# Address distance between TensorE's two operands in a decoder trunk: 64 bytes against 256 and 128, and the heads' outputs in the weights' class

## The chip, the cores and the metric

The kernel runs on one core of a Trainium2 chip. The time is that of one execution on the device, in microseconds; the median of three executions is given. One further execution was profiled, and all rows below come from it.

## The reference

Two post-norm layers on 512 tokens of width 1024, all in float32. Each layer is a half-step SwiGLU feed-forward network (FFN, hidden width 2816), a token mixer, a cross attention into 256 memory tokens, and a second FFN. Each of the four parts ends with a layer norm of `alpha * x + part`. The mixer of layer 0 is differential attention, that of layer 1 a causal pooling.

```python
for i in range(DEPTH):                                     # DEPTH = 2
    x = layer_norm(a * x + 0.5 * swiglu_ffn(x, ...), ...)
    h = diff_attention(x, ...) if i == 0 else pool_mixer(x, ...)
    x = layer_norm(a * x + h, ...)
    x = layer_norm(a * x + memory_cross_attention(x, mem, ...), ...)
    x = layer_norm(a * x + 0.5 * swiglu_ffn(x, ...), ...)
```

Differential attention has 8 heads with two 64-wide halves of queries and keys each, a rotary embedding, and for each head `softmax(first) - lambda * softmax(second)` times the values, normed per head, then a projection by `w_o`. The pooling mixer subtracts x from means over 2, 4, 8 or 16 past tokens and multiplies each group of 256 columns by its own 256x256 matrix. Cross attention has 4 heads of width 256 and a projection by `wo`.

## The kernel before

**One product is three passes.** TensorE works on float32r operands. Every float32 operand is split into a high part and a low part (`split`: ScalarE copies, VectorE subtracts), and a product is three matmul instructions: high by high, high by low, low by high. `mm3` issues them, its lines 220, 221 and 222. A matmul has a stationary operand, 128 by 128, that is loaded first, and a moving one of 128, 256 or 512 columns that streams through. In `mm3(out, w, x)` the stationary one is `w` and the moving one `x`. The profile names a matmul by output, moving tile, stationary tile: `q<-xh,wh` moves xh over stationary wh.

**Which operand is which.** In projections of x to transposed outputs (q, k of attention, xq of cross attention, the FFN's first products) the split weights wh and wl are stationary and the transposed activations xh and xl move. In products that give tokens as rows (v, pv, the pooling's products, the output projections in `to_tokens`) the activations or the heads' outputs oT are stationary and the weights move. `to_tokens` makes eight outputs (two halves of the width, four blocks of 128 tokens) of eight k steps each; the first four k steps take weights in wh and wl, the last four, in the last round, in tiles of other names that have become free: qk, low and p in attention, q and kv in cross attention.

**Where tiles lie.** All memory is laid out by pools that are opened one behind another, so that an address is the sum of what lies ahead. `run` opens the constants, the tokens X0 to X3 and small tiles, pads to 480 modulo 512 (`LINE`), and then opens `xt` with xh and xl. Nearly every tile is a multiple of 512 bytes per partition, so what is opened next starts at the same remainder. A stage opens its weights' pools by `stage_pools`, and ahead of wh a pad of `APART` = 64 bytes (`to_w`): the weights' class. Then `phase_pool` opens the stage's own tiles in the order of its arguments; the mark `_x` among them is a pad of 512 - 64 bytes (`to_x`), behind which tiles are again in x's class. Ahead of `_x` lie, in attention, low, rt, a, p, o and qk; behind it v, oT and mask. In the cross attentions pT, p and kv lie ahead (p and kv of the second are pools of its stage, kv in the weights' class), and q, oT and gb behind. In the pooling p, pw and gb lie ahead, pooled and sq behind. The memory's transposed tiles lie in x's class in both layers. X0 to X3 start at 160 modulo 512.

**What sets the order.** The order of TensorE's instructions is written out: `weave` runs a main generator (projections) and lets a side generator (scores, softmax, values of earlier heads) in by an estimated clock, and the Tile scheduler keeps a program order on each engine and adds the waits. Attention: `da_main` makes v, q and k head by head, `da_side` the scores (`sc`), the mixed and turned probabilities (`pt`) and the values (`po`, lines 1210 and 1211). Cross attention: `xa_main` makes memory keys (`pk`), memory values (`pv`) and queries (`xq`), `xa_head` scores (`xs`) and outputs (`xo`). Pooling: `pp` and the group products, which like those of `to_tokens` are named `ps`. Transposes (line 506 and others) take their data as stationary operand and move the identity.

The layer norm of a token block (`ln_token`, lines 380 to 395) reads two rows of gains, loaded in tiles of the phase (`gain`): hr and sr in the FFN, v in attention, gb in the cross attentions.

Of the kernel before, what the change touches and what calls it, by code (L numbers as in the profile page):

```python
# [58 lines left out]
TURNS = ((1, 2), (0, 3))  # L59


APART, ROUND, LINE = 64, 512, 480


INV_FREQ_BITS = (
# [54 lines left out]
class Trunk:  # L120
    def __init__(self, tc, a, out, upto=8):
        self.tc, self.nc, self.a, self.out, self.upto = tc, tc.nc, a, out, upto
        self.side, self.late, self.gates = [], [], []
        self.ln_next_gb, self.kv_bufs = None, 8


    def warm(self, tile, bank, n):
# [32 lines left out]

    def to_x(self, ctx):

        self.pad(ctx, ROUND - APART)

    def to_w(self, ctx):

        self.pad(ctx, APART)

    @contextmanager
    def phase_pool(self, gain, spare, **bufs):  # L170
# [1425 lines left out]
            yield from self.xa_head(*self.heads[h][1])  # L1596

    def cross_attention(self, layer, ln):
        bufs = dict(q=8, oT=10, gb=2)
        if layer == 0:  # L1600
            self.kv, self.keys = [], []
            late, mem = self.side_pool("mem"), self.side_pool("mem")
            with self.other_pools():
                self.stage["mem"], self.stage["late"] = mem, late
                with self.phase_pool(("gb", "gb"), "p", pT=6, p=4, kv=8, _x=0, **bufs):
                    self.kvp = self.phase["kv"]
                    with self.tc.high_priority():
                        self.load_memory("p")
                    self.turn_banks = None
                    self.xa(layer, ln)  # L1610
            self.close_side()
            self.close_side()
        else:
            with self.later, self.phase_pool(("gb", "gb"), "p", pT=6, p=4, _x=0, **bufs):
                self.xa(layer, ln)

    def xa(self, layer, ln):
# [51 lines left out]
        self.side.pop().__exit__(None, None, None)  # L1669

    def ffn_pools(self):
        return self.stage_pools(4, dict(ra=4, rc=3), ("wh", "wl", "ra", "rc"))

    def other_pools(self, order=("wh", "wl", "raw")):
# [19 lines left out]
            self.ffn(layer, 1, ln)  # L1694

    def mixer(self, layer, ln):
        if layer == 0:
            bufs = dict(low=4, rt=2, a=4, p=8, o=2, qk=8, _x=0, v=4, oT=11, mask=1)
            with self.other_pools(), self.phase_pool(("v", "v"), "rt", **bufs):
                self.diff_attention(layer, ln)  # L1700
            self.close_side()
        else:
            self.later = ExitStack()
            self.later.enter_context(self.stage_pools(4, dict(raw=2), ("wh", "wl", "mem", "p", "raw")))
            self.to_w(self.later)
            self.kvp = self.later.enter_context(self.pool("kv"))
            bufs = dict(p=4, pw=1, gb=2, _x=0, pooled=16, sq=1)
            with self.phase_pool(("gb", "gb"), "sq", **bufs):
                side = self.pool_mixer(layer, ln)
                with self.tc.high_priority():  # L1710
                    self.load_memory()
                w = self.a["xa_wkv"][layer]
                raws = [self.raw_cols(w, c) for c in (0, D)]
                self.pool_bias()
                next(side)
                self.kv, self.keys, self.kv_bufs = [], [], 10
                self.weave(self.early_kv(layer, ln, 2, raws), side, 850, 8500)
            self.close_side()
# [46 lines left out]
```

## Time and profile before

| | us |
|---|---|
| median of three executions | 1913.4 |
| lowest and highest | 1912.26 and 1915.36 |
| span of the profiled execution | 1913.0 |
| TensorE busy in it | 1894.9 |
| VectorE busy | 1550.6 |
| ScalarE busy | 1003.8 |
| attention, 339 to 580 us | 241 |
| first cross attention, 580 to 744 us | 164 |
| pooling and second cross attention, 1395 to 1582 us | 187 |

The four FFNs and the turns between stages fill the rest. In the rows of the profile, PE is TensorE's matmul, PEld its load of stationary operands, DVE VectorE, ACT ScalarE. A row that groups instructions gives line, engine, operation, output and inputs, shapes and count; behind the bar stand the busy time in us, the mean duration of one in ns, and the engine's idle time ahead of them. A row of the timeline starts with start and duration in us. The ends of matmuls are modelled, so that the step from one start to the next is what counts, not the share of busy time.

### The profile page before, as it was taken

Reading aid. Unit: us, or ns where it says so; the run is one execution under the profiler, and the core shown is the slowest. Engines: PE = TensorE matmul, PEld = TensorE weight load, DVE = VectorE, ACT = ScalarE, POOL = GpSimd, SP = SyncE. Lnnn points to the kernel's source line nnn. Section 1 sums busy time; section 2 is a strip of 40 time slices with the busy share of each in tenths; the row PEclk is TensorE's granted clock in tenths of the full one; section 3 lists DMA queues with packets and bytes.
Section 4 is the critical chain, followed back from the end, with each engine's and each line's share of the span. In section 5 each row is a group of like instructions: output and inputs, shape, how many; then the busy total and the mean of one; then the engine's idle time right before and its main releaser. Section 6 shows DMA issues by size and latency. Waiting matters only on the chain.

```text
span 1913.0 us, 32564 instructions
## 1 busy us (share of the span) xinstructions
PE 1894.9 (99%) x13136; PEld 1733.1 (91%) x13136; DVE 1550.6 (81%) x2250; ACT 1003.8 (52%) x1546; POOL 317.3 (17%) x274
## 2 busy tenths in 40 slices
PE   9999999999999999999999999999999999999998
PEld 8999998888878888999998999999899889999997
DVE  7888889888867558889888988898787568898886
ACT  6555554566645435645554655455455436555552
POOL 3112120111110001221220311212130012211210
PEclk9999999999999999999999999999999999999999
DMA  9978772323225327987785687878344438877861
GB/s 248 216 166 187 166 146 82 91 67 89 89 67 155 111 66 198 182 179 162 144 192 179 109 179 165 183 163 184 111 133 133 134 87 171 178 159 166 188 132 56
DMA packets 246743, 277.96 MB, mean 145 GB/s; under 512 B 8256, under 2 KB 212544, under 8 KB 246592
## 3 DMA queue, kind: packets, MB, share of 16 engines
q0 software_dynamic: 92928, 92.29, 31.5%
q1 hardware_dynamic: 153664, 183.59, 30.0%
q8 instruction: 103, 1.69, 0.4%
q14 instruction: 48, 0.39, 0.1%
HBM read 273.75 MB, written 2.10 MB: 144 GB/s over the span
## 4 chain that ended last, share of the span: by engine, by line
PE 85%; DVE 10%; ACT 2%; DMA 1%; issue 1%; POOL 1%; SPq 0%; DVEq 0%; ACTq 0%; POOLq 0%
PE x L221 7%; PE x L220 7%; PE x L222 7%; PE ps L220 4%; PE z L221 4%; PE z L220 4%; PE z L222 4%; PE ps L222 4%; PE ps L221 4%; PE px L222 2%; PE px L220 2%; PE px L221 2%; PE pt L506 2%; PE y L222 2%; PE x L757 2%; PE xq L222 2%
## 5 line engine op out<-in xcount | busy, mean ns | idle before, releaser
L725 POOL DMA_DIRECT2D ra<-in_ffn_w_in_dram x132 | 170.7, 1314 | 982.3 <-DVE wl L732 966.5
L730 ACT CAST wh<-ra 128x1024 fp32r<-128x1024 f32 x176 | 185.1, 1053 | 208.0 <-PE x L221 63.3
L732 DVE TENSOR_TENSOR wl<-ra,wh 128x1024 fp32r<-128x1024 f32 x176 | 214.4, 1223 | 66.5 <-ACT wh L730 66.1
L220 PE MATMUL x<-xe,wh 128*128 128x256 f32 x704 | 195.0, 277 | 0.0
L221 PE MATMUL x<-xe,wh 128*128 128x256 f32 x704 | 194.8, 277 | 0.0
L222 PE MATMUL x<-xe,wl 128*128 128x256 f32 x704 | 194.8, 277 | 0.0
L730 ACT CAST wh<-rc 128x1024 fp32r<-128x1024 f32 x132 | 139.0, 1053 | 102.4 <-PE x L221 41.6
L135 ACT CAST wh<-b 128x1024 fp32r<-128x1024 f32 x112 | 117.8, 1052 | 130.4 <-PE x L221 66.1
L732 DVE TENSOR_TENSOR wl<-rc,wh 128x1024 fp32r<-128x1024 f32 x132 | 160.3, 1222 | 25.5 <-ACT wh L730 25.5
L136 DVE TENSOR_TENSOR wl<-b,wh 128x1024 fp32r<-128x1024 f32 x112 | 136.9, 1222 | 41.0 <-ACT wh L135 41.0
L220 PE MATMUL x<-xh,wh 128*128 128x256 f32 x536 | 148.7, 277 | 0.0
L221 PE MATMUL x<-xl,wh 128*128 128x256 f32 x536 | 148.3, 277 | 0.0
L222 PE MATMUL x<-xh,wl 128*128 128x256 f32 x536 | 148.3, 277 | 0.0
L220 PEld LDWEIGHTS x<-xe,wh 128*128 128x128 f32 x704 | 132.4, 188 | 1.3
L221 PEld LDWEIGHTS x<-xe,wh 128*128 128x128 f32 x704 | 132.3, 188 | 1.3
L222 PEld LDWEIGHTS x<-xe,wl 128*128 128x128 f32 x704 | 132.2, 188 | 0.0
L136 DVE TENSOR_TENSOR wl<-raw,wh 128x1024 fp32r<-128x1024 f32 x64 | 82.4, 1296 | 41.1 <-ACT wh L135 40.5
L221 PEld LDWEIGHTS x<-xl,wh 128*128 128x128 f32 x536 | 100.8, 188 | 0.7
L220 PEld LDWEIGHTS x<-xh,wh 128*128 128x128 f32 x536 | 100.7, 188 | 0.7
L222 PEld LDWEIGHTS x<-xh,wl 128*128 128x128 f32 x536 | 100.6, 188 | 0.0
L135 ACT CAST wh<-raw 128x1024 fp32r<-128x1024 f32 x64 | 66.4, 1049 | 61.0 <-PE xq L221 19.1
L220 PE MATMUL z<-xe,wh 128*128 128x256 f32 x352 | 97.5, 277 | 0.0
(447 smaller groups left out, 6266.0 us busy)
## 6 DMA issues: line engine op xcount, KB each, us to landing
ra<-in_ffn_w_in_dram POOLq DMA_DIRECT2D x132, 512.0 KB, 7.0
rc<-in_ffn_w_in_dram SPq DMA_DIRECT2D x88, 512.0 KB, 5.8
b<-in_ffn_w_out_dram SPq DMA_DIRECT2D x76, 512.0 KB, 4.8
ra<-in_ffn_w_in_dram SPq DMA_DIRECT2D x44, 512.0 KB, 4.7
rc<-in_ffn_w_in_dram POOLq DMA_DIRECT2D x44, 512.0 KB, 7.8
raw<-in_xa_wkv_dram SPq DMA_DIRECT2D x16, 1024.0 KB, 5.4
raw<-in_da_w_qkv_dram SPq DMA_DIRECT2D x16, 512.0 KB, 5.2
raw<-in_xa_wq_dram SPq DMA_DIRECT2D x8, 1024.0 KB, 5.7
```

Source lines behind the costliest of these rows:

```text
L135: self.nc.scalar.copy(hi, src),
L136: self.nc.vector.tensor_sub(lo, src, hi.bitcast(F32)),
L220: self.first_mm = mm(out, w[0], x[0], start=start, stop=False, skip_group_check=again)
L221: mm(out, w[0], x[1], start=False, stop=False, skip_group_check=again)
L222: self.last_mm = mm(out, w[1], x[0], start=False, stop=stop, skip_group_check=again)
L506: self.turns = [self.nc.tensor.transpose(pt[:, j], b, self.ident) for j, b in enumerate(blocks)]
L725: nc.gpsimd.dma_start(t, source(*block), accum_op=ALU.add)
L730: hi = nc.scalar.copy(v[0], raw)
L732: lo = nc.vector.tensor_sub(v[1], raw, v[0].bitcast(F32))
L757: self.last_mm = nc.tensor.matmul(ps[:, j], v[i][:, k, j * P : (j + 1) * P], x[l][:, k], start=n == i == l == 0, stop=n == 7 and i == 1, s ...
```

## The change

The distance between the classes becomes a value of the stage: 64 bytes in the FFNs as before, 256 in attention and the first cross attention, 128 in the pooling and the second cross attention. The pad ahead of the weights has that size, and the pad back to x's class 512 bytes less it. Besides, oT is opened ahead of `_x` and not behind it, in attention and in both cross attentions, so that the heads' outputs lie in the weights' class; v (attention) and q (cross attentions) come to lie behind oT.

```diff
-APART, ROUND, LINE = 64, 512, 480
+APART, ROUND, LINE = dict(ffn=64, da=256, xa=(256, 128)), 512, 480
...
+        self.apart = APART["ffn"]
...
-        self.pad(ctx, ROUND - APART)
+        self.pad(ctx, ROUND - self.apart)
...
-        self.pad(ctx, APART)
+        self.pad(ctx, self.apart)
...
     def cross_attention(self, layer, ln):
-        bufs = dict(q=8, oT=10, gb=2)
+        bufs, self.apart = dict(_x=0, q=8, gb=2), APART["xa"][layer]
...
-                with self.phase_pool(("gb", "gb"), "p", pT=6, p=4, kv=8, _x=0, **bufs):
+                with self.phase_pool(("gb", "gb"), "p", pT=6, p=4, kv=8, oT=10, **bufs):
...
-            with self.later, self.phase_pool(("gb", "gb"), "p", pT=6, p=4, _x=0, **bufs):
+            with self.later, self.phase_pool(("gb", "gb"), "p", pT=6, p=4, oT=10, **bufs):
...
     def ffn_pools(self):
+        self.apart = APART["ffn"]
...
     def mixer(self, layer, ln):
+        self.apart = APART["xa"][1] if layer else APART["da"]
         if layer == 0:
-            bufs = dict(low=4, rt=2, a=4, p=8, o=2, qk=8, _x=0, v=4, oT=11, mask=1)
+            bufs = dict(low=4, rt=2, a=4, p=8, o=2, qk=8, oT=11, _x=0, v=4, mask=1)
```

No instruction is added or taken out, and none changes its shape.

## The prediction

> **What bounds the kernel now.** I read the page's head first, then the stages that the change touches (a table by windows), then single matmuls in order of time, then groups of matmuls by operands and shape.
>
> ```profile
> span 1913.0 us, 32564 instructions
> PE 1894.9 (99%) x13136; PEld 1733.1 (91%) x13136; DVE 1550.6 (81%) x2250; ACT 1003.8 (52%) x1546; POOL 317.3 (17%) x274
> PEclk9999999999999999999999999999999999999999
> PE 85%; DVE 10%; ACT 2%; DMA 1%; issue 1%; POOL 1%; SPq 0%; DVEq 0%; ACTq 0%; POOLq 0%
> ```
>
> TensorE is busy 99% of the span at its full granted clock, and 85% of the chain that ended last is its own. Time comes or goes only as its passes (one matmul instruction each) follow each other faster or slower. Attention runs from 339 to 580 us, the first cross attention to 744, pool and second cross attention from 1395 to 1582:
>
> ```profile
> 339.00:580.00 241.00, 236.44 (x1473) 200.76 (x1471) 190.90 (x470) 136.82 (x362) 40.69 (x54) 1.00 0.27 81
> 580.00:744.00 164.00, 163.38 (x977) 142.70 (x976) 98.40 (x156) 70.01 (x132) 7.25 (x6) 1.00 0.46 136
> 1395.00:1582.00 187.00, 186.06 (x1212) 167.60 (x1211) 131.21 (x204) 85.80 (x159) 21.62 (x15) 1.00 0.41 124
> ```
>
> Behind each window stand its length and TensorE's busy time: these 592 us are TensorE's too. The FFN stages keep their 64 bytes, so I cost them at nothing.
>
> The timeline shows what addresses can touch (start, duration, engine, line):
>
> ```profile
> 399.97 0.39 PE L220 MATMUL q<-xh,wh 128*128 128x512 f32 x1
> 399.97 0.19 PEld L221 LDWEIGHTS q<-xl,wh 128*128 128x128 f32 x1
> ...
> 419.75 0.39 PE L220 MATMUL k<-xh,wh 128*128 128x512 f32 x1
> ...
> 422.78 0.40 PE L221 MATMUL k<-xl,wh 128*128 128x512 f32 x1
> ```
>
> While a pass streams its moving operand (the first name behind the arrow), the load of the next pass's stationary operand (the second) begins: both read SBUF at once. What the change sets is their distance, the next stationary start less the present moving start, modulo 512. All slices of 128 columns are 512 bytes long, so it is one number for a pair of tiles. By the order and sizes of the pools, x's class starts at 480 modulo 512 and the weights' class 64 further on.
>
> The 13 steps from 419.75 to 422.78 take 233 ns each, at recorded durations that alternate between 0.39 and 0.40. A duration is the step plus some 163 ns, so differences of mean durations are differences of steps. The wide passes (512 columns), mean ns behind the bar; I take the second and third pass of each triple (L221, L222), since the first holds waits:
>
> ```profile
> L221 PE MATMUL q<-xl,wh 128*128 128x512 f32 x64 | 25.3, 396 | 0.0
> L222 PE MATMUL k<-xh,wl 128*128 128x512 f32 x64 | 25.3, 395 | 0.0
> L221 PE MATMUL xq<-xl,wh 128*128 128x512 f32 x112 | 44.2, 395 | 0.0
> L221 PE MATMUL ps<-wl,oT 128*128 128x512 f32 x96 | 37.7, 393 | 0.0
> L222 PE MATMUL ps<-wh,oT 128*128 128x512 f32 x96 | 37.7, 392 | 0.0
> L221 PE MATMUL ps<-q,oT 128*128 128x512 f32 x32 | 12.5, 390 | 0.0
> L222 PE MATMUL ps<-q,oT 128*128 128x512 f32 x32 | 12.4, 391 | 0.0
> L221 PE MATMUL ps<-ha,xe 128*128 128x512 f32 x30 | 11.7, 389 | 0.0
> L222 PE MATMUL ps<-ha,xe 128*128 128x512 f32 x1 | 0.4, 400 | 0.0
> L222 PE MATMUL ps<-kv,oT 128*128 128x512 f32 x1 | 0.4, 392 | 0.0
> ```
>
> Where x moves and weights are loaded (q, k, xq) the distance is +64: 395 to 396 ns. Where weights move and heads' outputs are loaded (wh or wl with oT) it is -64: 392 to 393. Where both lie in one class (q with oT, ha with xe) it is 0: 389 to 391. The last two rows are single passes followed by the load of a token tile X, which starts at 160: there the distance is +192 (ha with xe, 400) and +128 (kv with oT, 392). So distance costs up to 11 ns a pass. No pass of 512 or 256 columns with fp32 operands shows a distance of 256.
>
> The Trainium skill, page "TensorE: Matmul & The Clock Gate", section "Step-by-step: what each phase is for", says that TensorE reads moving and stationary operands through two independent ports, and that loading the next weights takes no read bandwidth from the running matmul. By it the sum below would be 0; the rows above speak against it.
>
> The narrow passes (256 columns):
>
> ```profile
> L221 PE MATMUL x<-xe,wh 128*128 128x256 f32 x704 | 194.8, 277 | 0.0
> L221 PE MATMUL v<-wl,xh 128*128 128x256 f32 x128 | 35.8, 280 | 0.0
> L221 PE MATMUL pv<-wl,mem2h 128*128 128x256 f32 x32 | 8.9, 278 | 0.0
> L221 PE MATMUL xs<-kv,q 128*128 128x256 f32 x64 | 17.8, 278 | 0.0
> L221 PE MATMUL ps<-wl,pooled 128*128 128x256 f32 x32 | 9.0, 282 | 0.0
> L221 PE MATMUL pk<-mem2l,wh 128*128 128x256 f32 x32 | 8.9, 278 | 0.0
> L221 PE MATMUL xq<-xl,wh 128*128 128x256 f32 x32 | 9.0, 282 | 0.0
> L222 PE MATMUL ps<-hb,xe 128*128 128x256 f32 x8 | 2.3, 284 | 0.0
> ```
>
> and two stretches of pk in the timeline:
>
> ```profile
> 605.84 0.28 PE L220 MATMUL pk<-mem4h,wh 128*128 128x256 f32 x1
> 606.90 0.28 PE L220 MATMUL pk<-mem6h,wh 128*128 128x256 f32 x1
> ...
> 635.84 0.28 PE L220 MATMUL pk<-mem6h,wh 128*128 128x256 f32 x1
> 636.97 0.28 PE L221 MATMUL pk<-mem2l,wh 128*128 128x256 f32 x1
> ```
>
> Among the groups the order is another one: +64 is best in the FFN (277), -64 gives 278 to 282, and 0, the best for wide passes, is worst (284). The timeline warns against a finer reading: the same operands at +64 run nine steps in 1.06 us (118 ns) at 606 us and ten in 1.13 (113 ns) at 636. A stretch of narrow passes falls into one of two paces and stays there.
>
> **The change part by part.** Durations are from the profiled execution, 1913.0 us, against the 1913.4 of the median; I subtract from the median.
>
> Heads' outputs into the weights' class. to_tokens makes 3 x 8 x 8 x 3 = 576 wide passes in the three stages. In 480 of them (all of attention's, and wh, wl and kv in both cross attentions) moving and stationary now share a class: from -64 to 0. From 392.5 to 390.3 is -2.2 ns, x 480 = -1.1 us; bounds 0 and -3.5 ns (to 389), 0 to -1.7 us.
>
> The other 96, those of the tiles q, go from 0 to +256 or +128. Between 389 and 400 I take 393.5, +3 ns, near the 392 row: +0.3 us (bounds -0.1 to +0.9).
>
> q, k and xq: 192 + 192 in attention and 192 in the first cross attention go from +64 to +256, 144 in the second to +128: 720 wide passes at 395.4. Bounds are the best and the worst row, 389 and 400: -4.6 us to +3.3 us. I take 391.5. For +128 that is the row of 392. For 256 nothing is measured; it is the furthest apart that two starts can be modulo 512, and three of the five measured distances lie at 389 to 393. -3.9 x 720 = -2.8 us.
>
> The narrow passes: 384 of v, 384 of pv, 192 of xs and 96 of pooled leave -64 for 256 or -128; 384 of pk and 96 of xq leave +64 for +256 or +128. 1536 passes at 279.3 in the mean of their rows, between 277 and 284: -3.5 us to +7.2 us. Since pace depends on how a stretch is entered, I take little, -0.5 ns, near the bulk of rows at 278 to 280: -0.8 us.
>
> ```profile
> L1210 PE MATMUL po<-v,a 128*128 128x256 f32 x80 | 20.0, 312 | 0.0
> L1211 PE MATMUL po<-v,a 128*128 128x128 f32 x80 | 17.8, 223 | 0.0
> ```
>
> ```profile
> 343.12 1.28 DVE L395 SCALAR_TENSOR_TENSOR X<-X,rstd,sr 128x1024 f32<-128x1024 f32 x1
> 345.42 0.59 ACT L135 CAST v<-v 128x512 fp32r<-128x512 f32 x1 [0.72 <-PE v L222]
> ```
>
> po goes from +64 to +256 in 160 passes, too few to matter: 0, at 5 ns either way 0.8 us. Scores (q and k in one class) and xo (pT and kv in one class) keep distance 0.
>
> Tiles also move. In attention oT now lies ahead of v, so v lands 22 KB higher, where the FFN kept its norm's gains (tiles sr and hr). The first write of v on ScalarE would wait for the last read of sr on VectorE; that read ends at 344.40 and the write starts at 345.42, so it costs nothing with 1.0 us to spare. Were that cover gone, ScalarE's split of the weights behind it would come late, and TensorE with it, by at most the norm's 1.28 us. In the cross attentions q and oT change places over tiles read for the last time some 10 us earlier or more. No instruction, DMA or wait is added.
>
> Sum: -1.1 + 0.3 - 2.8 - 0.8 = -4.4 us, 1909.0.
>
> **The rivals.** First, all passes reach the best rows: -1.7 - 0.1 - 4.6 - 3.5 = -9.9, 1903.5. For it: 277 and 389 exist under load. Against: no distance gives both.
>
> Second, no change. Either distances count modulo 256 only: then 256 acts as 0, 576 wide passes gain 5.1 ns (-2.9), 864 narrow ones (v, pk, pv and xs of the first two stages) go to 284, +5 ns (+4.3), and with -1.1 for the heads' outputs it is +0.3, 1913.7. Or address distance is not the cause of the steps, or the pads don't produce it: 1913.4. For the former: the narrow and wide orders oppose each other at 0. Against: +192 and -64 would be the same, and they show 400 and 392. Against the latter: the same moving tile, ha, takes 389 or 400. The latter is what the two-port rule of the Trainium skill, page "TensorE: Matmul & The Clock Gate", comes to; the trace does not agree, by these 11 ns.
>
> Third, slower: the weight load sets the pace of narrow passes. A recorded load (0.19 above) is longer than the step of 113 to 120, so a load that is held up delays the next pass at once, while a wide pass has twice the time to hide it. If both new distances hold it up as 0 does now, 1536 passes go to 284: +7.2, and with wide passes unimproved +7.2 - 1.1 + 0.3 = +6.4, 1919.8. It decides once narrow passes lose 0.5 ns in the mean without a gain in the wide ones, or 2.3 ns with it. For it: 284 at 0. Against: 113 ns steps occur at +64 whatever runs beside.
>
> **How the numbers follow.** Forecast 0.50, first rival 0.12, second 0.26 (0.06 of it for steps that addresses do not set), third 0.12. A change of 0.2%, 3.8 us, is about what can be told from none. The forecast's own range is -7 to -1.5 us, two thirds of it beyond 3.8: faster 0.33 + 0.12 = 0.45, same 0.17 + 0.26 = 0.43, slower 0.12. The range takes in the first rival, the second and the forecast and leaves out the third: 1903.5 to 1914.5; the forecast alone 1906.4 to 1911.9.
>
> **What would show it.** In the groups of the changed kernel: wh and wl with oT at 389 to 391; q, k, xq at 391 to 392, not 395; pk, pv, v, xs at 277 to 280. The three windows should be shorter by about 2.5 us (attention), 1 (first cross attention) and 1 (second). Narrow rows at 282 to 285 would mean the third rival; wide rows still at 395 the second. A gap ahead of the first v copy would mean the moved tiles cost.

## The result: 1923.6 us, slower by 0.6%

| | before | after |
|---|---|---|
| median, us | 1913.1 | 1923.57 |
| lowest and highest | 1910.59 and 1915.36 | 1922.39 and 1925.2 |
| ratio, 95% interval | | 1.0058 [1.0046, 1.0070] |
| span of the profiled execution | 1913.0 | 1923.4 |
| attention, first pass of v to first of pk | 241.0 | 247.9 |
| first cross attention, from there to the first FFN pass | 164.2 | 168.2 |
| the two FFNs between | 650.7 | 650.8 |
| pooling and second cross attention | 186.7 | 187.2 |

The forecast was 1909.0, with a range from 1903.5 to 1914.5. The change costs some 11 us, and nearly all of it lies in attention and the first cross attention. (The stages grow by 11.5 us and the span by 10.4, since the first FFN, in which nothing was changed, took 1.3 us less in this execution; over the runs below it took 336.5 to 340.7.) The head of the page after:

```profile
span 1923.4 us, 32565 instructions
PE 1897.3 (99%) x13136; PEld 1739.9 (90%) x13136; DVE 1551.1 (81%) x2250; ACT 1003.7 (52%) x1546; POOL 317.4 (17%) x274
PEclk9999999999998999999999999999999999999999
```

TensorE's busy time rose by 2.4 us only, while the span rose by 10.4: most of the loss is idle time. And one slice of the granted clock, the thirteenth (577 to 625 us), shows an 8 where before it showed 9. Both point to the turn between attention and cross attention. The stages by windows (length, TensorE's busy time, and so on to the clock, DMA's share and GB/s):

```profile
337.90:585.80 247.90, 235.62 (x1471) 201.33 (x1468) 197.31 (x477) 138.50 (x366) 41.85 (x55) 0.99 0.27 84
585.80:754.00 168.20, 166.54 (x977) 147.68 (x977) 92.78 (x148) 68.65 (x128) 6.56 (x6) 0.98 0.42 126
```

In attention 12.3 us are now without a pass, 4.6 before. The timeline of before and then of after at that turn:

```profile
579.53 0.60 PE L1452 MATMUL pt<-ident,p 128*128 128x128 f32 x4
579.57 0.59 ACT L135 CAST mem4h<-pt 128x512 fp32r<-128x512 f32 x1
...
580.21 0.38 PE L220 MATMUL pk<-mem4h,wh 128*128 128x256 f32 x1
```

```profile
578.12 0.60 PE L1453 MATMUL pt<-ident,p 128*128 128x128 f32 x4
...
582.48 1.28 DVE L394 SCALAR_TENSOR_TENSOR X<-X,mean,v 128x1024 f32<-128x1024 f32 x1
...
583.86 1.28 DVE L396 SCALAR_TENSOR_TENSOR X<-X,rstd,v 128x1024 f32<-128x1024 f32 x1
585.18 0.58 ACT L136 CAST mem4h<-pt 128x512 fp32r<-128x512 f32 x1 [3.38 <-DVE X L396]
...
585.82 0.58 PE L221 MATMUL pk<-mem4h,wh 128*128 128x256 f32 x1 [7.10 <-ACT mem4h L136]
...
591.20 0.41 PE L222 MATMUL pk<-mem2l,wh 128*128 128x256 f32 x1
591.41 0.41 PE L223 MATMUL pk<-mem2h,wl 128*128 128x256 f32 x1
591.62 0.37 PE L221 MATMUL pk<-mem4h,wh 128*128 128x256 f32 x1
591.83 0.28 PE L222 MATMUL pk<-mem4l,wh 128*128 128x256 f32 x1
591.95 0.29 PE L223 MATMUL pk<-mem4h,wl 128*128 128x256 f32 x1
```

The cross attention begins with the memory's transposed tiles: TensorE turns the memory (pt), ScalarE copies the high part (mem4h), and pk multiplies it. Before, the copy starts 0.04 us after the transposes do. After, it starts 7.06 us after them, and the row says what released it: VectorE's line 396, the end of the last token block's norm, which reads the gains in tiles named v. The addresses say why. The memory's tiles are laid from the far end of SBUF: mem0h from 212960, mem4h from 221152. Before, oT filled 199648 to 222176, and v, with the gains in it, ended at 199648. After, v lies behind oT: the gains g from 205792 and b from 218080 to 222176. So mem4h may not be written until b has been read for the last time. The scheduler moved the copies behind the whole norm of the last token block (before, the first step of that norm on ScalarE came 3.4 us after the first copy), and TensorE stood still for 7.10 us.

The second loss follows. The passes behind the gap start 0.21 us apart, and from 591.83 on 0.12: for nearly 6 us TensorE ran at half its pace, on 24 passes or so, 24 x 0.09 = 2.2 us. The granted clock (the third number from the end) shows it in this window:

```profile
581.60:591.80 10.20, 5.83 (x25) 5.54 (x26) 7.08 (x8) 3.35 (x7) 1.08 (x1) 0.50 0.89 305
```

The clock fell to half 2.9 us after the end of the last transpose and came back 10.2 us later; the 8 in its row is this. What else the cross attention lost of its 4.0 us is a wait of 1.5 us ahead of a pass of kv with oT, which is 0 to 0.6 us in the three other runs of this order (e2, e5, e6), and the passes' own steps, below. The Trainium skill, page "TensorE: Matmul & The Clock Gate", section "HAM oscillation — how this bites in real kernels", tells of TensorE falling to half rate after an idle gap of over some 3.4 us; the trace agrees as to the half rate, with a gap of 7.10 us and steps of 0.21 against 0.12, but here the clock fell before 3.4 us had passed, at 2.9.

What the change was about can be read from the groups of after, the second and third pass of a triple (now L222 and L223):

```profile
L222 PE MATMUL xq<-xl,wh 128*128 128x512 f32 x112 | 43.9, 392 | 0.0
...
L222 PE MATMUL ps<-wl,oT 128*128 128x512 f32 x96 | 37.6, 391 | 0.0
...
L222 PE MATMUL v<-wl,xh 128*128 128x256 f32 x128 | 36.2, 283 | 0.0
...
L223 PE MATMUL k<-xh,wl 128*128 128x512 f32 x64 | 25.2, 393 | 0.0
L222 PE MATMUL q<-xl,wh 128*128 128x512 f32 x64 | 25.1, 392 | 0.0
...
L222 PE MATMUL xs<-kv,q 128*128 128x256 f32 x64 | 18.1, 282 | 0.0
...
L223 PE MATMUL ps<-q,oT 128*128 128x512 f32 x32 | 12.6, 393 | 0.0
...
L222 PE MATMUL ps<-wl,pooled 128*128 128x256 f32 x32 | 9.1, 285 | 0.0
...
L222 PE MATMUL pv<-wl,mem2h 128*128 128x256 f32 x32 | 9.0, 282 | 0.0
```

The wide passes came near the forecast: q, k and xq at 391 to 393, not 395 to 396. The mean of xq hides two stages, though: by windows it went from 395 and 397 to 390 and 391 in the first cross attention (256 bytes), and only from 394 and 395 to 394 in the second (128 bytes). The narrow ones did not: v went from 280 to 283, xs and pv from 278 to 282, pooled from 282 to 285.

### The profile page after: what moved, and what is told of

It reads as the page before. It is cut to its first block, busy times and chain, and to the rows that moved or that the text cites. A ratio compares the mean times of both kernels' runs of the same rounds, so it can differ in the third digit from the quotient of the medians.

```text
span 1923.4 us, 32565 instructions
## 1 busy us (share of the span) xinstructions
PE 1897.3 (99%) x13136; PEld 1739.9 (90%) x13136; DVE 1551.1 (81%) x2250; ACT 1003.7 (52%) x1546; POOL 317.4 (17%) x274
## 4 chain that ended last, share of the span: by engine, by line
PE 85%; DVE 9%; ACT 2%; DMA 2%; issue 1%; POOL 1%; SPq 0%; DVEq 0%; ACTq 0%; POOLq 0%
PE x L222 7%; PE x L221 7%; PE x L223 7%; PE z L222 4%; PE z L221 4%; PE z L223 4%; PE ps L221 4%; PE ps L223 4%; PE ps L222 4%; PE px L221 2%; PE px L223 2%; PE px L222 2%; PE y L223 2%; PE pt L507 2%; PE xq L221 2%; PE xq L223 2%
## 5 line engine op out<-in xcount | busy, mean ns | idle before, releaser
L222 PE MATMUL x<-xe,wh 128*128 128x256 f32 x704 | 194.8, 277 | 0.0
L223 PE MATMUL x<-xe,wl 128*128 128x256 f32 x704 | 194.8, 277 | 0.0
L136 ACT CAST wh<-b 128x1024 fp32r<-128x1024 f32 x112 | 117.8, 1052 | 131.5 <-PE x L222 67.0
L222 PE MATMUL x<-xl,wh 128*128 128x256 f32 x536 | 148.4, 277 | 0.0
L223 PE MATMUL x<-xh,wl 128*128 128x256 f32 x536 | 148.4, 277 | 0.0
L222 PEld LDWEIGHTS x<-xe,wh 128*128 128x128 f32 x704 | 132.3, 188 | 1.4
L223 PEld LDWEIGHTS x<-xe,wl 128*128 128x128 f32 x704 | 132.2, 188 | 0.0
L222 PEld LDWEIGHTS x<-xl,wh 128*128 128x128 f32 x536 | 100.7, 188 | 0.7
L223 PEld LDWEIGHTS x<-xh,wl 128*128 128x128 f32 x536 | 100.6, 188 | 0.0
```

Source lines behind the costliest of these rows:

```text
L136: self.nc.scalar.copy(hi, src),
L222: mm(out, w[0], x[1], start=False, stop=False, skip_group_check=again)
L223: self.last_mm = mm(out, w[1], x[0], start=False, stop=stop, skip_group_check=again)
```

## The experiments

Two theories at the start. **Wait:** the tiles' new order costs the 7 us gap and the half pace behind it, and distances nearly cancel. **Distance:** the new distances themselves make passes slower, and the gap is only where it shows.

| run | what it is | ratio to before, 95% interval | attention | first cross attention |
|---|---|---|---|---|
| change | | 1.0058 [1.0046, 1.0070] | 247.9 | 168.2 |
| e1_v_low | change, v below oT | 1.0007 [0.9998, 1.0015] | 240.9 | 164.7 |
| e2_order_alone | change's order, 64 bytes | 1.0049 [1.0035, 1.0062] | 247.9 | 165.6 |
| e3_distance_alone | change's distances, old order | 1.0013 [1.0004, 1.0021] | 241.0 | 165.3 |
| e4_layer0_256 | e1, 64 bytes in layer 1 | 1.0005 [0.9997, 1.0014] | 240.9 | 166.5 |
| e5_gains_swapped | change, g and b changed over | 1.0045 [1.0032, 1.0059] | 246.5 | 166.8 |
| e6_warm_wait | change, TensorE busy in the gap | 1.0041 [1.0028, 1.0053] | 248.0 | 165.0 |
| e8_all64_v_low | e1 with 64 bytes | 1.0000 [0.9991, 1.0008] | 241.0 | 164.2 |
| e9_192 | e8 with 192 bytes | 1.0005 [0.9996, 1.0014] | 239.9 | 164.5 |
| e10_192_ffn | e9, FFN's ha and hb moved | 1.0090 [1.0076, 1.0104] | 240.2 | 163.8 |

**e1_v_low** keeps the new distances and oT in the weights' class, but lays v where nobody needs the room early; `_w` is a pad back to the weights' class.

```diff
-            bufs = dict(low=4, rt=2, a=4, p=8, o=2, qk=8, oT=11, _x=0, v=4, mask=1)
+            bufs = dict(low=4, rt=2, a=4, p=8, o=2, _x=0, v=4, _w=0, qk=8, oT=11, mask=1)
```

> The change with one more pad, so that v (which also holds the gains of attention's norm) lies below qk and oT and away from the memory's transposed tiles; classes and distances are those of the change in all stages. Wait theory (the 10 us are a wait of the memory's first transposed tile for the norm's last reading of the gains in v, 7 us, and passes at half clock behind it, 2 us): both go, 1914 us, and the first pk pass starts within 1.5 us of attention's last transposes. Distance theory (narrow passes at 256 and 128 cost the 10 us): 1922 to 1924, unchanged.

1914.06 us, ratio 1.0007 [0.9998, 1.0015]. The gap is gone; the turn in the timeline:

```profile
576.70 0.60 PE L1455 MATMUL pt<-ident,p 128*128 128x128 f32 x4
576.74 0.59 ACT L136 CAST mem4h<-pt 128x512 fp32r<-128x512 f32 x1
...
577.38 0.39 PE L223 MATMUL pk<-mem4h,wh 128*128 128x256 f32 x1
```

That the place of v costs the time is shown, for attention and for what the half pace took behind it.

**e2_order_alone** is the complement: the change's order with 64 bytes everywhere.

```diff
-APART, ROUND, LINE = dict(ffn=64, da=256, xa=(256, 128)), 512, 480
+APART, ROUND, LINE = dict(ffn=64, da=64, xa=(64, 64)), 512, 480
```

> The change with 64 bytes in every stage: only the places of oT, v and q are those of the change. Wait theory: 1921 to 1923, with the same wait of 7 us ahead of pk and half-clock passes behind it. Distance theory: 1912 to 1913, as the kernel before or 1 us better for the heads' outputs at distance 0.

1922.79 us: the order alone brings 9.4 of the change's 11.1 us (0.0049 and 0.0058 of 1913). Attention takes the change's 247.9 us, and the gap is the same to 0.01 us:

```profile
586.97 0.58 PE L221 MATMUL pk<-mem4h,wh 128*128 128x256 f32 x1 [7.10 <-ACT mem4h L136]
```

**e3_distance_alone**: 256, 256 and 128 bytes in the old order, oT still in x's class.

```diff
-APART, ROUND, LINE = 64, 512, 480
+APART, ROUND, LINE = dict(ffn=64, da=256, xa=(256, 128)), 512, 480
...
-        bufs = dict(q=8, oT=10, gb=2)
+        bufs, self.apart = dict(_x=0, q=8, oT=10, gb=2), APART["xa"][layer]
```

> The change with oT behind x's pad again, as before: only the distances 256 and 128 are those of the change. Wait theory: no wait ahead of pk, 1913 to 1915; q, k, xq of layer 0 some 5 ns a pass faster, narrow passes 2 to 5 ns slower, which cancels. Distance theory: 1922 to 1924.

1915.6 us, +2.5 (0.8 to 4.0). The distances alone cost a little where the prediction has a gain (-2.8 for q, k and xq, -0.8 for the narrow passes). The groups show both halves of it, a wide one better than before by 4 and a narrow one worse by 4:

```profile
L222 PE MATMUL q<-xl,wh 128*128 128x512 f32 x64 | 25.1, 392 | 0.0
...
L222 PE MATMUL xs<-kv,q 128*128 128x256 f32 x64 | 18.1, 282 | 0.0
```

**e4_layer0_256** is e1_v_low with `xa=(256, 64)`, so that pooling and second cross attention have their old distance.

> As e1, but 64 bytes in the pooling and second cross attention, with oT in the weights' class there too. Wait theory: 1 us below e1, since at 128 narrow passes cost 2 ns more than at 64 and wide ones gain only 1: 1912 to 1913. Distance theory: halfway between before and the change, 1917 to 1919.

1914.11 us against e1's 1914.06. The stage itself got shorter, 186.8 against 187.2 us, but the first cross attention took 1.8 us longer, with a gap of 1.0 us ahead of an xq pass (for VectorE's wl) and one of 0.7 ahead of kv with oT. Nothing of the edit lies there; such gaps at the end of a split come and go between runs, and they are larger than what was to be seen. Inconclusive as to the microsecond.

**e5_gains_swapped** asks whether it is the overlap of these very tiles: b is loaded first, so that g, which the norm reads one step earlier, lies under mem4h.

```diff
-        for t, n in zip(got, ("ln_g", "ln_b")):
+        order = -1 if self.gain[0] == "v" else 1
+        for t, n in list(zip(got, ("ln_g", "ln_b")))[::order]:
```

> The change with the order of the two loads of gains turned round in attention's norm, so that the first-read gains (g) and not the last-read ones (b) lie in the slot of v that mem4h is laid over. Wait theory: the first copy of mem4h then waits for VectorE's last reading of g instead of b, 1.4 us earlier by the profile of the change (the reading of g ends at 583.76, of b at 585.14), so the wait ahead of pk shrinks from 7.1 to 5.7 us, 1922 us. Rival, that the wait is for the end of the norm as such or for the banks of the transposes: no difference, 1923.6.

The time is 1922.28 us, as expected. The copy now waits for the reading of g (line 395 here, 394 in the change), and the gap is 1.40 us shorter, which is the step from one reading to the other (583.86 - 582.48 = 1.38 in the change):

```profile
583.46 0.59 ACT L136 CAST mem4h<-pt 128x512 fp32r<-128x512 f32 x1 [1.99 <-DVE X L395]
...
584.09 0.58 PE L221 MATMUL pk<-mem4h,wh 128*128 128x256 f32 x1 [5.70 <-ACT mem4h L136]
```

**e6_warm_wait** adds 30 wide passes over xh into a bank that nobody reads, behind the memory's transposes.

```diff
+        if tag:
+            bank, x = self.aux("idle", "px"), self.xh[0]
+            with self.tc.issue_after(turned.ins):
+                for _ in range(30):
+                    nc.tensor.matmul(bank, x[:, 2, :P], x[:, :2, : 2 * P], start=True, stop=True)
```

> The change with 30 wide passes that nobody reads, in the wait ahead of pk, so that TensorE is not idle in it. If the passes at 0.21 us behind the wait are TensorE's clock, lowered by the idle time, they run at 0.12 us from the first and the time falls by 2.2 us to 1921.4. If they are the late splits of memory's tiles, the steps stay at 0.21 and the time at 1923.6. The wait itself stays at 7 us in both.

The wait stays (attention 248.0 us), but the passes behind it start 0.12 us apart at once, and the first cross attention takes 165.0 us instead of 168.2 (0.9 of it because the wait ahead of kv with oT is 0.6 us here and 1.5 in the change):

```profile
586.50 0.29 PE L221 MATMUL pk<-mem4h,wh 128*128 128x256 f32 x1
586.62 0.28 PE L222 MATMUL pk<-mem4l,wh 128*128 128x256 f32 x1
586.74 0.28 PE L223 MATMUL pk<-mem4h,wl 128*128 128x256 f32 x1
```

The clock does not fall here. So the half pace comes from standing idle. Its price, 2.2 us in the timeline, fits the times (1921.86 against 1923.57, each from five runs), whose difference of 1.7 is at the edge of what they tell apart.

**e7_distance_sweep** measures the disputed cost by itself. It leaves the trunk out: chains of 96 passes of one width and one distance, nothing else running but a copy of each result. Its time, 840.8 us, says nothing of the kernel.

> Leaves out the whole trunk: chains of 96 matmuls on copies of x, one operand at distances 0, 32, 64, 128, 192, 256, 320, 384 and 448 from the other modulo 512, wide (w) twice and narrow (n) four times; no other engine works beside them. Theory (the two reads of TensorE get in each other's way by their distance): wide steps 227 ns at 0 and 256 and 229 to 237 elsewhere, 64 and 192 worst; narrow steps 120 at 0 and 256, 119 at 128, 113 to 118 at 64. If distance counts modulo 256, 320 is as 64 and 384 as 128. Rival (steps are set by other engines' accesses, the distance only coincides): one step for all distances, 227 and 113.

From the first to the last start of a chain, by windows (95 steps each): wide at 0, 64, 128, 192 and 256; then narrow at 64, at 256, and at 64 once more, in a descending order of distances:

```profile
24.86:46.39 21.53, 21.53 (x96) 17.83 (x95) 0.00 (x0) 0.00 (x0) 0.00 (x0) 1.00 0.00 1
69.02:91.19 22.17, 22.17 (x97) 17.86 (x95) 0.69 (x1) 0.00 (x0) 0.00 (x0) 1.00 0.00 0
91.42:113.50 22.08, 22.08 (x96) 17.90 (x95) 0.69 (x1) 0.00 (x0) 0.00 (x0) 1.00 0.00 1
113.73:135.47 21.74, 21.74 (x96) 17.84 (x95) 0.69 (x1) 0.00 (x0) 0.00 (x0) 1.00 0.00 1
135.71:157.25 21.54, 21.54 (x96) 17.83 (x95) 0.69 (x1) 0.00 (x0) 0.00 (x0) 1.00 0.00 1
247.02:258.21 11.19, 11.19 (x97) 11.19 (x96) 0.42 (x1) 0.00 (x0) 0.00 (x0) 1.00 0.01 1
281.03:292.42 11.39, 11.39 (x97) 11.39 (x96) 0.42 (x1) 0.00 (x0) 0.00 (x0) 1.00 0.00 0
796.82:807.59 10.77, 10.77 (x98) 10.77 (x96) 0.43 (x1) 0.00 (x0) 0.00 (x0) 1.00 0.01 2
```

The steps, as means over the chains of a kind:

| step, ns | 0 | 32 | 64 | 128 | 192 | 256 | 320 | 384 | 448 |
|---|---|---|---|---|---|---|---|---|---|
| wide | 226.7 | 233.3 | 233.3 | 232.4 | 228.9 | 226.9 | 233.3 | 232.4 | 228.9 |
| narrow | 120.0 | 118.3 | 117.8 or 113.3 | 118.6 | 117.8 or 113.3 | 120.0 | 117.8 or 113.3 | 118.7 | 117.8 |

The table repeats after 256 bytes: 256 is 0 to these passes. Wide passes are best at 0, narrow ones worst; 192, expected among the worst for wide passes, is the next best. And the narrow chain at 64 took 117.8 ns a step in ascending order and 113.3 in descending order, twice each. The sweep moves the stationary tile only, so that alone it can't tell that tile's distance from its place. The trunk can: in e8_all64_v_low below, weights that are the stationary tile and heads' outputs that are the stationary tile start at one place modulo 512, and the passes take 395 to 396 ns where x moves over the weights (64) and 391 to 392 where weights move over the heads' outputs (0).

**e8_all64_v_low** is e1_v_low with 64 bytes everywhere: only the heads' outputs in the weights' class.

> 64 bytes in every stage, oT in the weights' class in all three and v low as in e1: the heads' outputs at distance 0 alone, without the wait. Theory: 1 us better than before, 1912. Rival, that the distance of oT is worth nothing here: 1913.

1913.44 us, ratio 1.0000 [0.9991, 1.0008]. The passes of weights with oT take 391.6 ns in the mean instead of 392.4, which is 0.4 us in 480 passes, and half a microsecond can't be seen in the time.

**e9_192** and **e10_192_ffn** use the sweep: 192 is the best distance that leaves narrow passes alone, and the FFN's down passes (px, py, pz) could go to 0.

```diff
-APART, ROUND, LINE = dict(ffn=64, da=64, xa=(64, 64)), 512, 480
+APART, ROUND, LINE = dict(ffn=64, da=192, xa=(192, 192)), 512, 480
```

> The order of e8_all64_v_low (heads' outputs in the weights' class, v below, no wait), with 192 bytes instead of 64 in attention, pool and both cross attentions. If the sweep's law holds in the kernel, the 720 wide passes of q, k and xq go from about 233 ns a step at 64 to 228.9 at 192, -4.5 x 720 = -3.2 us; the passes with heads' outputs stay at 0, and narrow passes stay where they are, since 192 and -192 leave the two paces of 64: 1909.5 to 1910.5, about 0.998 of the kernel before, and durations of q, k and xq of about 391 instead of 395. If what single passes gain is taken up again by waits for splits, copies or landings further on, the durations fall as said, but the time stays at 1913 and the gaps grow. If the law of a chain with nothing else running doesn't carry over to a loaded memory, q, k and xq stay at 394 to 396 and the time at 1913.

```diff
-        bufs = dict(b1=1, b3=1, b2=1, b4=1, _x=0, xe=6, hb=4, sp=4, ha=4, sr=1, hr=3)
+        bufs = dict(b1=1, b3=1, b2=1, b4=1, hb=4, ha=4, _x=0, xe=6, sp=4, sr=1, hr=3)
```

> e9_192 and, besides, hb and ha of the four FFNs laid into the weights' class, 64 bytes on as before: the wide down passes whose weights move over stationary tiles of ha and hb go from -64 to 0, some 1344 passes at 2 to 2.5 ns, -3 us, while some 270 passes of the last round, whose moving tile already shared a class with ha and hb, lose about 2 ns, +0.6 us: 1907 to 1908, about 0.997, and some 2.5 us below e9_192, all of it in the FFN stages. If the gains are taken up by waits (the FFN waits for weights' landings and splits), the FFN stages keep 337, 650 and 331 us and the time is that of e9_192. If laying the tiles anew brings a new write-after-read wait, as it did in the change, a gap of a microsecond or more stands at one of the stage's ends and the time is above e9_192.

e9_192 took 1914.32 us, no gain where 3 us were expected, although q, k and xq went to 391 to 394. Attention is 1.1 us shorter than before and layer 1's stage 0.7, but in the profiled execution the last FFN, in which nothing was changed, took 334.9 us instead of 331.3. The windows from 1590 to 1640 of before and of e9_192, narrow FFN passes only, tell why (the number behind TensorE's busy time counts its passes):

```profile
1590.00:1640.00 50.00, 50.00 (x441) 49.91 (x440) 43.89 (x48) 33.18 (x42) 13.85 (x11) 1.00 0.94 192
```

```profile
1590.00:1640.00 50.00, 50.00 (x427) 50.00 (x426) 42.66 (x49) 30.84 (x39) 14.16 (x11) 1.00 1.00 202
```

441 passes or 427 in the same 50 us, with no idle time in either: these are the sweep's two paces, 113 and 117 ns a step. In e9_192 the slow pace held until 1710 us. Whether it did so in the other executions is not on record; their times, 1912.7 to 1916.4, differ by as much.

e10_192_ffn took 1930.92 us, slower by 0.9% where a gain of 0.3% was expected. Its down passes did what was expected (394 and 392 before), and the FFN's narrow passes, whose distance is untouched, fell into the slow pace (277 before):

```profile
L223 PE MATMUL x<-xe,wh 128*128 128x256 f32 x704 | 197.3, 280 | 0.0
...
L225 PE MATMUL px<-wh,hb 128*128 128x512 f32 x192 | 74.8, 389 | 0.0
L224 PE MATMUL px<-wl,hb 128*128 128x512 f32 x192 | 74.7, 389 | 0.0
```

Over all groups of the four FFNs, 1344 down passes gained 2.3 ns, 3.1 us, and 7392 narrow ones lost 3.2 ns, 23 us. Attention, cross attentions and pooling gained 2.3 us. 23.4 - 3.1 - 2.3 makes 18, and 17.0 were measured. No wait was added.

**e11_entry** asks what decides the pace. It leaves the trunk out as well: the same 96 narrow passes at 64 behind seven kinds of passes, in three orders.

> It leaves out the trunk. 96 narrow passes at a distance of 64, always the same, stand behind seven kinds of passes: 24 wide ones at 0 (a), 64 (b), 128 (c) or 192 (d), 48 narrow ones at 0 (e) or 128 (f), or 3 wide ones at 0 (g), in three different orders (x, y, z). The sweep showed 117.8 or 113.3 ns a step at 64 by what stood ahead. If the last passes ahead decide the pace, each kind gives the same pace in all three orders: 113.3 behind d, whose distance is that of the FFN's wide passes, and 117.8 behind a, as in the FFN of e10_192_ffn. If the pace is carried over from further back, the same kind gives 113.3 in one order and 117.8 in another, above all a and g, whose passes at 0 all take 226.7 and shift nothing. If the pace had to do with the memory's other users, which are all absent here, all 21 stretches would go at one pace.

Rows of the chains at 64 (after), by order (x, y, z) and kind, and two of the wide chain at 192 that stood ahead (in):

```profile
L36 PE MATMUL ydafter<-mov,st 128*128 128x256 f32 x96 | 11.5, 281 | 0.0
...
L36 PE MATMUL xfafter<-mov,st 128*128 128x256 f32 x96 | 11.1, 276 | 0.0
...
L36 PE MATMUL xdafter<-mov,st 128*128 128x256 f32 x96 | 11.1, 276 | 0.0
L36 PE MATMUL zdafter<-mov,st 128*128 128x256 f32 x96 | 11.1, 276 | 0.0
...
L36 PE MATMUL ydin<-mov,st 128*128 128x512 f32 x24 | 5.8, 397 | 0.0
...
L36 PE MATMUL xdin<-mov,st 128*128 128x512 f32 x24 | 5.7, 391 | 0.0
```

Behind wide passes at 192 (d) the passes took 276 ns in two orders (113 a step) and 281 in the third (118), and in the third the wide passes themselves took 397 instead of 391. Behind wide passes at 0 (a) and narrow ones at 0 (e) it was 281 in all three, behind narrow ones at 128 (f) 276 in all three; behind b, c and g it depended on the order. So the kind ahead doesn't decide alone, something is carried over from further back, and the memory's other users are not needed for it. What it is that is carried over stays open. That the stretches of 24 or 48 passes at 0 were followed by the slow pace each time (not the three passes of g) agrees with e10_192_ffn, whose down passes stand at 0.

## Why the prediction was wrong

**The step that failed** is the one on the moved tiles. It said that v lands 22 KB higher, checked who had the new place last (the FFN's gains, 1.0 us to spare), and closed: "No instruction, DMA or wait is added." A tile that is moved has two neighbours in time: who used its new place before it, and who is to use it after. The second was not looked up. It is the memory's tiles, laid from the far end of SBUF, and they are on TensorE's path at once, since pk is the first product of the next stage. The prediction looked for "a gap ahead of the first v copy"; the gap stood at the other end of the stage. Nor did any rival have a wait in it. e1_v_low, e2_order_alone and e5_gains_swapped show this cause, at 6.9 us of attention, and e6_warm_wait that of the half pace behind it, 2.2 us by the timeline.

**The sum by its terms**, means of the second and third passes, from the rounded rows of all groups of a kind (pk by e1_v_low, where no half pace is in it):

| term | passes | before, ns | after, ns | forecast, us | by the rows, us |
|---|---|---|---|---|---|
| weights with oT, -64 to 0 | 480 | 392.4 | 391.6 | -1.1 | -0.4 |
| q with oT, 0 to 256 or 128 | 96 | 390.5 | 392.5 | +0.3 | +0.2 |
| q, k, xq, 64 to 256 or 128 | 720 | 395.4 | 391.9 | -2.8 | -2.5 |
| narrow, ±64 to 256 or 128 | 1536 | 279.2 | 282.9 | -0.8 | +5.7 |
| sum | | | | -4.4 | +3.0 |

e1_v_low measured +1.3 (-0.4 to +2.9) and e3_distance_alone +2.5. Of the wide terms that of q, k and xq held as a sum, in e1's kernel as in the change, by luck: 256 was taken for the furthest apart and is the same as 0, and at 128, where the row of a single pass stood for 144, they gained 0.5 ns and not 3. That of the heads' outputs came to a third of its size. The narrow term was mis-sized, with the wrong sign: the bounds, 277 and 284, held, and the choice near the bulk of rows had no ground, since 256 had a row as soon as 256 and 0 are the same.

**That they are the same** was in the second rival ("distances count modulo 256 only", narrow passes to 284, priced at +0.3 us), and was argued away because 192 and -64 would then be the same, but showed 400 and 392. They are the same: the row of 192 passes at -64 was right (chains at 192 take 228.9 ns a step, 2.2 above those at 0), and the 400 was a single pass ahead of a transpose's load. A count of one, with another kind of instruction behind it, was no row for a chain; nor was the 392 at 128, where chains take 232.4. As to distances the second rival was right for 256, and the third, narrow passes at 282 to 285, for the size of their loss; its price of +6.4 us assumed wide passes that do not gain, and they do.

**The Trainium skill's two ports** (page "TensorE: Matmul & The Clock Gate", section "Step-by-step: what each phase is for") would have all these steps alike. The sweep disagrees, with no other engine at work: 226.7 to 233.3 ns for wide passes by the distance alone, and for narrow ones 113.3 to 120.0 by the distance and by what ran ahead.

**Right** were what bounds the kernel, and that addresses can bring little: no version here beat the kernel before by what can be measured. The chance of "slower", 0.12, rested on one mechanism, and the one that decided was not among the rivals. One working was off besides: of a range of -7 to -1.5 us, 0.58 lies beyond -3.8 and not two thirds, which would have made "faster" 0.41 and not 0.45.

## What to carry to other kernels

When a tile moves, list for its new place the last user before and the first user after, on both sides of a stage's end and from both ends of the memory; the second can sit at the head of the next stage, where nothing covers its wait. A wait on TensorE can cost more than its length: behind those of 5.7 and 7.1 us here the passes ran at half pace, behind those of up to 1.5 us they did not. Take the price of a pass from a chain of its own kind, and ask of a small gain per pass whether the passes behind it keep their pace.

## What the runs showed of the hardware

- What counts is the distance modulo 256 bytes: 0 and 256, 64 and 320, 128 and 384 give the same steps to some 0.3 ns, as long as a narrow chain is in the same one of its paces.
- Wide passes are best at 0 (226.7 ns), narrow ones worst (120.0, where 64 and 192 reach 113.3). Which end of the range is best thus depends on the width.
- At 64 and 192 narrow passes have two paces, 113.3 and 117.8 ns, and wide ones at 192 too (228.9 and 233.3). The slow pace held over 110 us of the trunk at a stretch. It depends on what ran ahead, further back than the last chain, and 7392 FFN passes at 3.2 ns made 23 us of it.
- In a gap of 7.1 us the granted clock fell to 0.50 after 2.9 us and stayed there for 10.2 us, of which nearly 6 were passes at half pace. In e5_gains_swapped, with a gap of 5.7 us, it fell after some 2 us and stayed as long. 30 passes that nobody reads kept it up (e6_warm_wait).
